# Layer modulation and gates on VectorE: two contraction tiles by 1024 columns at a time, with the sums over partitions two ticks later

## The chip, the cores and the metric

One Trainium2 chip, of which the kernel uses one core. The metric is device time in microseconds (us) of one execution. Engines are called by their profile names: PE (TensorE matmul), PEld (its weight load), DVE (VectorE), ACT (ScalarE), POOL (GpSimd), SP (the queue that issues most loads).

## The reference, cut to what matters

The model has two layers over 256 tokens of width 2048, all in float32. Each layer takes a shift, a scale and a gate from one conditioning vector, and uses them so (only the latent path is shown; the context path has its own first-layer modulation):

```python
def modulation(cond, w, b, n):
    m = jax.nn.silu(cond) @ w[:, :n * D_MODEL] + b[:n * D_MODEL]
    return jnp.split(m, n, axis=-1)

for i in range(DEPTH):
    sh, sc, gt = modulation(c_lat, w_ada[i], b_ada[i], 3)
    u = x * (1.0 + sc) + sh
    y = even_mixer(u @ w_in_e, ...) if i == 0 else odd_mixer(u @ w_in_o, ...)
    x = layer_norm(alpha * x + gt * y, ln_g[i], ln_b[i])
```

`w_ada` has 2048 rows (the contraction) and 6144 columns per layer: shift, scale, gate, 2048 each. A product with a single vector uses each weight once, so it is 16 MB of loads per section and little arithmetic.

## The kernel before, in words

The heavy products run as three matmuls each (`mm3`, L188): a weight tile is split by ACT (L152) and DVE (L153) into a high and a low float32r part, so that each 1 MB weight unit costs two ACT casts and two DVE subtractions of 128x1024. Weight units are four contraction tiles of 128 by 512 columns, loaded by SP (`load_unit`, L135) into a ring of four raw buffers of 4 KB per partition; `w_ahead` (L165) loads up to two units ahead and splits one ahead.

The stages, with the times that the profile shows for them: first-layer modulation and keys (0 to 198 us), values V (198 to 276), queries and the first gate (276 to 376), eight convolution blocks (376 to 602; the gated linear attention runs beside them), first output product OE with its layer norm (602 to 718), second layer's product ODD (718 to 903), second output product OO with the last norm (903 to 1004).

Four sections of 2048 columns are the subject here: `c` (second layer's scale), `g` (first layer's gate), `h` (second layer's shift), in this order (`ADA_ORDER`, L34), and after OE the second layer's gate, `gt1` (L1194). None uses PE for the contraction. DVE multiplies a weight tile [128, 512] by the conditioning value of each partition and adds it to an accumulator `aacc` (`ada_accum`, L525): one tensor_scalar (L531) for the first tile, 15 scalar_tensor_tensor (L533) for the rest of a block of 512 columns. A 1 MB unit is four contraction tiles by 512 columns, from the same raw ring, by the same SP queue. When a block of 512 is complete, PE sums over partitions: for `c` and `h` four matmuls against a column of ones (L554) and a bias add on DVE (L293, L295); for the gates a matmul against a matrix of ones (L520) and an add (L521) to a tile `gt` into which POOL loaded the bias when the block began (L513).

Who sets the pace: sections are generators. After each weight unit of a heavy product `tick` (L608) is called; it runs what was deferred to `later`, advances background work, and adds a stage's credit to a counter, and each whole credit advances the front generator by one `yield`:

```python
ada_credit[0] += ada_credit[1]
pump_ada(int(ada_credit[0]))
ada_credit[0] -= int(ada_credit[0])
```

Credits per tick are 3 in V (6 ticks), 0.4 in the 16 ticks of queries and first gate, 0.8 in the 32 ticks of the convolution blocks, 1 in OE (12 ticks before its last block) and 0.55 in ODD (36 ticks). A block of 512 columns has five yields, four of which each load a unit; a section has four blocks, so 20 yields. ODD's ticks come in this order: g0 (4), x0 (4), x1 (4), p0 (1), x2 (4), p1 (1), x3 (4), p2 (1), g1 (4), p3 (1), g2 (4), g3 (4). Blocks x take 20 matmuls per tick, the others 24.

`cols_ab` (L1133) and the line after `drain()` at the end of ODD (L1334) force what is left; `add` in `ln_blocks` (L1078) forces the gates that it needs. The order of instructions on each engine is set at build time by a list scheduler that goes by program order as priority and by modelled durations, so an instruction can stand some way from its place in the program; at run time each engine keeps its order and waits at the head of its queue. Most large tiles share one pool `s4` of `NSLOT` = 31 slots of 4 KB per partition; `gt` is one of them, `aacc` is not (a pool of its own, two buffers of 2 KB).

Of the kernel before, what the change touches and what calls it, by code (L numbers as in the profile page):

```python
# [21 lines left out]
NSLOT = 31  # L22
# [4 lines left out]
ADA_SLOT = None  # L27
ADA_PE = ((), ())
# [7 lines left out]
ADA_PRIO = 0  # L36
# [10 lines left out]
ADA_ENG = ("v", "v", "v", "v")  # L47
# [13 lines left out]
def kernel(  # L61
# [403 lines left out]
    def ENG(names):  # L465
        return names and [{"v": nc.vector, "g": nc.gpsimd}[n] for n in names]

# [10 lines left out]
    def ada_unit(layer, k0, n0):  # L478

        if not ADA_SLOT:  # L480
            r = load_unit(w_ada[layer], k0, 4, n0)
            return [r[:, j, :] for j in range(4)]
        q = {"s": nc.sync, "g": nc.gpsimd}[ADA_SLOT]
        parts = []
        for k in (k0, k0 + 2):
            r = slot([P, 2, 512], F32, "araw")
            q.dma_start(r, w_ada[layer][k * P : (k + 2) * P, n0 : n0 + 512].rearrange("(k p) n -> p k n", p=P))
            parts += [r[:, 0, :], r[:, 1, :]]
        return parts

    def ada_acc_gen(layer, n0, hold):
        ps = mp([P, 512], "adl")
        for k0 in range(0, KT, 4):
            r = ada_unit(layer, k0, n0)
            for j in range(4):
                nc.tensor.matmul(
                    out=ps[32 * j : 32 * j + 32, :], lhsT=sil[:, k0 + j, 2:34], rhs=r[j],
                    start=k0 == 0, stop=k0 == KT - 4)
            if k0 < KT - 4:
                yield  # L500
        hold.append(ps)
        yield
# [3 lines left out]
    def ada_rows_gen(layer, dst, engs):  # L506

        for nb in range(4):
            if nb % 2 == 0:
                dst.append(slot([P, 2, 512], F32, "gt"))  # L510
            g = dst[nb // 2][:, nb % 2, :]
            n0 = 2 * D + nb * 512
            nc.gpsimd.dma_start(g, b_ada[layer : layer + 1, n0 : n0 + 512].to_broadcast([P, 512]))  # L513
            a = small([P, 512], "aacc1")
            for k0 in range(0, KT, 4):
                ada_accum(ada_unit(layer, k0, n0), k0, a, engs)
                if k0 == KT - 4:
                    yield
                    pb = mp([P, 512], "gtb")
                    nc.tensor.matmul(out=pb, lhsT=ones, rhs=a, start=True, stop=True)  # L520
                    nc.vector.tensor_tensor(out=g, in0=pb, in1=g, op=ALU.add)  # L521
                    gt_done.setdefault(id(dst), set()).add(nb)
                yield

    def ada_accum(r, k0, a, engs):  # L525
        e = engs[(k0 // 4) % len(engs)]
        with prio(ADA_PRIO):
            for j in range(4):
                sc = sil[:, k0 + j, 2:3]
                if k0 + j == 0:  # L530
                    e.tensor_scalar(out=a, in0=r[j], scalar1=sc, scalar2=None, op0=ALU.mult)  # L531
                else:
                    e.scalar_tensor_tensor(out=a, in0=r[j], scalar=sc, in1=a, op0=ALU.mult, op1=ALU.add)  # L533

    def ada_cols_gen(layer, n0, dst, bias, one, engs, on_pe=()):

        for nb in range(4):
            ns = slice(4 * nb, 4 * nb + 4)
            if nb in on_pe:
                hold = []  # L540
                for _ in ada_acc_gen(layer, n0 + nb * 512, hold):
                    if not hold:
                        yield
                add_bias(dst[:, ns], to_cols(hold[0], 512)[:, :, 0], bias[:, ns], one)
                yield
                continue
            a = small([P, 512], "aacc1")
            for k0 in range(0, KT, 4):
                ada_accum(ada_unit(layer, k0, n0 + nb * 512), k0, a, engs)
                yield  # L550
            yield
            pt = mp([P, 4], "adaS")
            for q in range(4):
                nc.tensor.matmul(out=pt[:, q : q + 1], lhsT=a[:, q * P : (q + 1) * P], rhs=ones[:, 0:1], start=True, stop=True)  # L554
            add_bias(dst[:, ns], pt, bias[:, ns], one)

    gt0, gt1 = [], []
    jobs = {
        "c": lambda: ada_cols_gen(1, D, scT1, bT[1][:, 16:32], True, ENG(ADA_ENG[0]), ADA_PE[0]),
        "h": lambda: ada_cols_gen(1, 0, shT1, bT[1][:, 0:16], False, ENG(ADA_ENG[1]), ADA_PE[1]),  # L560
        "g": lambda: ada_rows_gen(0, gt0, ENG(ADA_ENG[2])),
# [39 lines left out]
    later = []  # L601

    def flush():
        now, later[:] = later[:], []
        for f in now:
            f()
# [464 lines left out]
    def ln_blocks(src, order, getu, res, gt, budget, after, before=None, between=None, halves=False):  # L1071
# [3 lines left out]
        def add(nb, m, cs=slice(0, 512)):  # L1075
            if nb not in rt:
                rt[nb] = res(nb)
            while ada_bg and not (len(gt) > nb // 2 and nb in gt_done.get(id(gt), ())):  # L1078
                pump_ada(1)
# [107 lines left out]
    def x1_gen():  # L1187
        for nb in range(4):
            for row, op in ((ln_g[0], ALU.mult), (ln_b[0], ALU.add)):
                t = bcast_row(row, nb)  # L1190
                nc.vector.tensor_tensor(out=rt[nb], in0=rt[nb], in1=t.unsqueeze(1).to_broadcast([P, 2, 512]), op=op)
                yield 1200

    ada_bg.append(ada_rows_gen(1, gt1, ENG(ADA_ENG[3])))  # L1194
    ada_credit[1] = ADA_1
    B = 2500

# [183 lines left out]
```

## Time and profile before

| what | value |
|---|---|
| runs of the kernel, median (lowest to highest) | 1011.63 us (1009.72 to 1018.11), 3 runs |
| the profiled execution | 1005.89 us |
| its span of instructions | 1004.1 us |
| granted TensorE clock, mean | 0.995 |

The profile is of one execution. Its span is 1.8 us shorter than that execution's time; the execution itself is 5.7 us below the median. Matmuls are pipelined and their ends are modelled, so a PE that shows as fully busy can still have small holes.

### The profile page before, as it was taken

What the parts mean: (1) busy time and instruction counts of PE and PEld (TensorE: products, weight loads), DVE (VectorE), ACT (ScalarE), POOL (GpSimd) and SP (SyncE); (2) the same over time, 40 slices, a digit from 0 to 9 for tenths busy, and PEclk for the clock granted to TensorE, in tenths of its full rate; (3) what the DMA queues carried; (4) which work ended last, traced back from release to release, by engine and by line L of the source; (5) the groups of instructions that cost most, each with busy time, mean ns of one, the idle gap of its engine ahead of it and who ended that gap; (6) DMA issues with size and microseconds to landing.
All of it is one profiled execution on the core that took longest, in us unless ns stands there. A gap on an engine that the chain in (4) does not pass through costs nothing.

```text
span 1004.1 us, 14346 instructions
## 1 busy us (share of the span) xinstructions
PE 958.9 (95%) x5654; PEld 757.0 (75%) x5654; DVE 807.0 (80%) x1172; ACT 468.9 (47%) x643; POOL 24.4 (2%) x56
## 2 busy tenths in 40 slices
PE   5899999999999999999999999999989999989995
PEld 4566756778878877877888788888778777768885
DVE  1555646989996999799999879997979997666676
ACT  2422214356675676246463344345745555435340
POOL 2000000000000000000000000000010001000000
PEclk9999999999999999999999999999999999999998
DMA  9987899567787586757766897985598998875532
GB/s 264 328 263 257 289 290 339 188 242 235 260 300 262 179 268 218 257 195 258 248 215 226 299 309 263 327 303 200 175 354 288 309 333 317 264 282 190 178 117 84
DMA packets 150371, 255.44 MB, mean 254 GB/s; under 512 B 5078, under 2 KB 46720, under 8 KB 150304
## 3 DMA queue, kind: packets, MB, share of 16 engines
q1 hardware_dynamic: 146592, 245.13, 72.5%
q0 software_dynamic: 2896, 8.72, 2.9%
q8 instruction: 44, 0.72, 0.3%
q10 hardware_dynamic: 816, 0.68, 0.3%
q14 instruction: 23, 0.19, 0.0%
HBM read 252.41 MB, written 2.10 MB: 253 GB/s over the span
## 4 chain that ended last, share of the span: by engine, by line
PE 49%; DVE 29%; DMA 15%; issue 4%; ACT 2%; SPq 0%; DVEq 0%; ACTq 0%
DMA raw<-in_w_ada_dram 12%; DVE wl L153 10%; DVE aacc L533 7%; PE oacc L190 5%; PE oacc L191 5%; PE oacc L192 5%; PE xacc L192 5%; PE xacc L191 5%; PE xacc L190 5%; PE ada L274 2%; DMA raw<-in_w_in_o_dram 2%; PE kacc L190 2%; PE kacc L192 2%; PE kacc L191 2%; PE pr L405 1%
## 5 line engine op out<-in xcount | busy, mean ns | idle before, releaser
L152 ACT CAST wh<-raw 128x1024 fp32r<-128x1024 f32 (+1 forms) x250 | 257.2, 1044 | 249.4 <-PE xacc L192 74.5
L153 DVE TENSOR_TENSOR wl<-raw,wh 128x1024 fp32r<-128x1024 f32 (+1 forms) x250 | 298.0, 1210 | 46.7 <-ACT wh L152 44.2
L533 DVE SCALAR_TENSOR_TENSOR aacc<-raw,sil,aacc 128x512 f32<-128x512 f32 x240 | 179.3, 747 | 30.8 <-DMA raw<-in_w_ada_dram 27.1
L190 PE MATMUL xacc<-wh,uxh 128*128 128x512 f32 x384 | 152.6, 397 | 0.0
L192 PE MATMUL xacc<-wh,uxl 128*128 128x512 f32 x384 | 151.5, 395 | 0.0
L191 PE MATMUL xacc<-wl,uxh 128*128 128x512 f32 x384 | 150.2, 391 | 0.5 <-DVE wl L153 0.4
L191 PEld LDWEIGHTS xacc<-wl,uxh 128*128 128x128 f32 x384 | 72.2, 188 | 16.3 <-DVE wl L153 1.3
L190 PEld LDWEIGHTS xacc<-wh,uxh 128*128 128x128 f32 x384 | 72.1, 188 | 15.5 <-ACT wh L152 0.5
L192 PEld LDWEIGHTS xacc<-wh,uxl 128*128 128x128 f32 x384 | 72.1, 188 | 15.3 <-issue 0.2
L425 DVE TENSOR_TENSOR knat<-kacc,knat 128x512 f32<-128x512 f32 x64 | 42.8, 685 | 34.7 <-PE kacc L192 34.5
L285 ACT COPY arow<-ada 128x256 f32<-128x256 f32 (+1 forms) x9 | 3.1, 349 | 100.6 <-PE ada L274 100.6
L274 PE MATMUL ada<-raw,sil 128*32 128x256 f32 (+1 forms) x576 | 36.2, 382 | 10.8 <-DMA raw<-in_w_ada_dram 10.8
L190 PE MATMUL xacc<-wh,u1h 128*128 128x512 f32 x112 | 44.9, 401 | 0.8 <-ACT u1h L1160 0.8
L190 PE MATMUL oacc<-wh,y1h 128*128 128x512 f32 (+1 forms) x120 | 45.5, 379 | 0.0
L191 PE MATMUL xacc<-wl,u1h 128*128 128x512 f32 x112 | 44.7, 399 | 0.5 <-DVE wl L153 0.4
L192 PE MATMUL oacc<-wh,y1l 128*128 128x512 f32 (+1 forms) x120 | 45.0, 375 | 0.0
L191 PE MATMUL oacc<-wl,y1h 128*128 128x512 f32 (+1 forms) x120 | 45.0, 375 | 0.0
L192 PE MATMUL xacc<-wh,u1l 128*128 128x512 f32 x112 | 44.5, 397 | 0.0
L274 PEld LDWEIGHTS ada<-raw,sil 128*32 128x32 f32 x576 | 17.4, 118 | 27.0 <-issue 12.0
L190 PE MATMUL kacc<-wh,uxh 128*128 128x512 f32 x64 | 26.8, 418 | 1.5 <-ACT uxh L397 1.5
L1221 PE MATMUL xacc<-wh,dm 128*128 128x512 f32 x64 | 25.7, 402 | 2.5 <-ACT wh L152 2.5
L190 PE MATMUL kacc<-wh,uch 128*128 128x512 f32 x64 | 26.4, 412 | 0.5 <-DVE knat L425 0.5
(339 smaller groups left out, 1866.6 us busy)
## 6 DMA issues: line engine op xcount, KB each, us to landing
raw<-in_w_ada_dram SPq DMA_DIRECT2D x96, 1024.0 KB, 6.3
raw<-in_w_in_e_dram SPq DMA_DIRECT2D x54, 1024.0 KB, 5.5
raw<-in_w_in_o_dram SPq DMA_DIRECT2D x32, 1024.0 KB, 7.2
raw<-in_w_out_e_dram SPq DMA_DIRECT2D x16, 1024.0 KB, 7.0
raw<-in_w_out_o_dram SPq DMA_DIRECT2D x16, 1024.0 KB, 5.1
raw<-in_w_in_e_dram SPq DMA_DIRECT2D x18, 512.0 KB, 7.0
raw<-in_w_pool_dram SPq DMA_DIRECT2D x4, 1024.0 KB, 7.7
gt<-in_b_ada_dram POOLq DMA_DIRECT2D x8, 256.0 KB, 4.1
```

The source lines that it names most:

```text
L152: nc.scalar.copy(h, r[:, j : j + w, :])
L153: nc.vector.tensor_tensor(out=l, in0=r[:, j : j + w, :], in1=h.bitcast(F32), op=ALU.subtract)
L190: nc.tensor.matmul(out=acc, lhsT=uh, rhs=wh, start=start, stop=False)
L191: nc.tensor.matmul(out=acc, lhsT=uh, rhs=wl, start=False, stop=False)
L192: nc.tensor.matmul(out=acc, lhsT=ul, rhs=wh, start=False, stop=stop)
L274: nc.tensor.matmul(out=ps[32 * g : 32 * g + 32, :], lhsT=sil[:, kt, 2 - 2 * half : 34 - 2 * half], rhs=r[:, j, :], start=half == 0 and kt ...
L285: arow_ins.append(nc.scalar.copy(a[:, :nw], ps))
L405: nc.tensor.matmul(out=pr[32 * g : 32 * g + 32, :], lhsT=wr[:, kk, :], rhs=quad_u[kk // 2][:, kk % 2, :], start=True, stop=True,)
L425: nc.vector.tensor_tensor(out=dst, in0=acc, in1=dst, op=ALU.add)
L533: e.scalar_tensor_tensor(out=a, in0=r[j], scalar=sc, in1=a, op0=ALU.mult, op1=ALU.add)
L1221: nc.tensor.matmul(out=accs[0], lhsT=dh, rhs=wh, start=f, stop=False)
```

## The change

The four sections are rewritten. A unit is two contraction tiles by 1024 columns instead of four by 512 (the same 1 MB, the same ring and queue), and DVE works on 128x1024 at a time. A section is two halves of 1024 columns with eight units and eight yields each, 16 yields instead of 20; the credits are unchanged. When a half is complete, its sums over partitions are put off by two ticks (two weight units): `finish` then issues, for a gate, the slot for `gt`, both bias loads on POOL, both matmuls and both adds; for a scale or shift, eight matmuls and one bias add. The accumulator is now one 4 KB slot of `s4`, and `NSLOT` goes from 31 to 32. `ada_end` replaces the forcing at L1135 and L1334, and `add` waits for `gt_done` by running `flush` once the generators are exhausted. The other removed functions (`ada_unit`, `ada_acc_gen` and their options) were not used with the options set.

```diff
-NSLOT = 31
+NSLOT = 32
...
+    def after_ticks(n, f):
+        later.append(f if n == 0 else lambda: after_ticks(n - 1, f))
...
+    def ada_section(layer, n0, finish):
+
+        for half in range(2):
+            c0 = n0 + half * 1024
+            a = slot([P, 1024], F32, "aacc")
+            for k0 in range(0, KT, 2):
+                r = load_unit(w_ada[layer], k0, 2, c0, 1024)
+                for j in range(2):
+                    sc = sil[:, k0 + j, 2:3]
+                    if k0 + j == 0:
+                        nc.vector.tensor_scalar(out=a, in0=r[:, j, :], scalar1=sc, scalar2=None, op0=ALU.mult)
+                    else:
+                        nc.vector.scalar_tensor_tensor(out=a, in0=r[:, j, :], scalar=sc, in1=a, op0=ALU.mult, op1=ALU.add)
+                if k0 == KT - 2:
+                    ada_open[0] += 1
+                    after_ticks(2, lambda half=half, a=a: finish(half, a))
                 yield
...
+    def ada_end():
+        pump_ada(1000)
+        while ada_open[0]:
+            flush()
+
+    def ada_rows_gen(layer, dst):
+
+        def finish(half, a):
+            dst.append(slot([P, 2, 512], F32, "gt"))
+            for i in range(2):
+                nb, g = 2 * half + i, dst[half][:, i, :]
+                n0 = 2 * D + nb * 512
+                nc.gpsimd.dma_start(g, b_ada[layer : layer + 1, n0 : n0 + 512].to_broadcast([P, 512]))
+                pb = mp([P, 512], "gtb")
+                nc.tensor.matmul(out=pb, lhsT=ones, rhs=a[:, i * 512 : (i + 1) * 512], start=True, stop=True)
+                nc.vector.tensor_tensor(out=g, in0=pb, in1=g, op=ALU.add)
+                gt_done.setdefault(id(dst), set()).add(nb)
+            ada_open[0] -= 1
+
+        return ada_section(layer, 2 * D, finish)
+
+    def ada_cols_gen(layer, n0, dst, bias, one):
+
+        def finish(half, a):
+            ns = slice(8 * half, 8 * half + 8)
+            pt = mp([P, 8], "adaS")
+            for q in range(8):
                 nc.tensor.matmul(out=pt[:, q : q + 1], lhsT=a[:, q * P : (q + 1) * P], rhs=ones[:, 0:1], start=True, stop=True)
             add_bias(dst[:, ns], pt, bias[:, ns], one)
+            ada_open[0] -= 1
+
+        return ada_section(layer, n0, finish)
```

## Rows read from the trace of the kernel before

**Rows 1.** The page's first part: busy us, share of span, instructions of each engine.
```profile
PE 958.9 (95%) x5654; PEld 757.0 (75%) x5654; DVE 807.0 (80%) x1172; ACT 468.9 (47%) x643; POOL 24.4 (2%) x56
```

**Rows 2.** Windows by stage: length, PE, PEld, DVE, ACT, POOL, clock, DMA share, GB/s.
```profile
198.00:276.00 78.00, 77.58 (x353) 63.84 (x352) 71.63 (x104) 46.66 (x72) 0.51 (x5) 1.00 0.73 251
276.00:376.00 100.00, 98.39 (x740) 79.44 (x739) 91.03 (x118) 68.39 (x82) 1.41 (x5) 1.00 0.75 252
376.00:602.00 226.00, 220.46 (x1588) 179.40 (x1588) 206.43 (x319) 110.13 (x148) 3.96 (x6) 1.00 0.74 247
602.00:690.00 88.00, 87.62 (x408) 72.54 (x407) 80.54 (x109) 37.59 (x43) 0.00 (x0) 1.00 0.83 291
718.00:903.00 185.00, 176.69 (x786) 143.11 (x785) 152.87 (x187) 93.14 (x114) 10.10 (x20) 0.99 0.88 302
...
940.00:960.00 20.00, 20.00 (x90) 16.57 (x89) 12.11 (x15) 7.74 (x8) 0.00 (x0) 1.00 0.60 191
```

**Rows 3.** The same windows, tile aacc alone: length, PE, PEld, DVE, clock, DMA, GB/s.
```profile
198.00:276.00 78.00, 2.85 (x24) 3.15 (x24) 35.62 (x50) 1.00 0.73 251
276.00:376.00 100.00, 1.97 (x10) 1.42 (x10) 18.83 (x26) 1.00 0.75 252
376.00:602.00 226.00, 4.19 (x14) 1.94 (x14) 58.40 (x80) 1.00 0.74 247
602.00:690.00 88.00, 2.95 (x24) 2.98 (x24) 23.30 (x32) 1.00 0.83 291
...
718.00:903.00 185.00, 3.14 (x6) 0.97 (x6) 46.78 (x64) 0.99 0.88 302
```

**Rows 4.** Waits of PE: us in total, times, longest us.
```profile
PE yT L968 <- DVE y L962: 4.1, 3, 2.0
PE y1T L1279 <- DVE gate L1326: 3.3, 1, 3.3
...
PE xacc L1221 <- ACT wh L152: 2.5, 1, 2.5
...
PE gtb L520 <- DVE aacc L533: 0.3, 1, 0.3
...
PE adaS L554 <- DVE aacc L533: 0.2, 1, 0.2
```

**Rows 5.** Groups of DVE by form: count, busy us, mean ns, idle before and releaser.
```profile
L153 DVE TENSOR_TENSOR wl<-raw,wh 128x1024 fp32r<-128x1024 f32 x246 | 295.3, 1219 | 45.9 <-ACT wh L152 43.4
L533 DVE SCALAR_TENSOR_TENSOR aacc<-raw,sil,aacc 128x512 f32<-128x512 f32 x240 | 179.3, 747 | 30.8 <-DMA raw<-in_w_ada_dram 27.1
L425 DVE TENSOR_TENSOR knat<-kacc,knat 128x512 f32<-128x512 f32 x64 | 42.8, 685 | 34.7 <-PE kacc L192 34.5
...
L531 DVE TENSOR_SCALAR aacc<-raw,sil 128x512 f32<-128x512 f32 x16 | 7.7, 479 | 9.6 <-DMA raw<-in_w_ada_dram 9.6
```

**Rows 6.** Timeline of DVE, then of PE, late in ODD: start, us, idle before.
```profile
881.28 0.75 DVE L533 SCALAR_TENSOR_TENSOR aacc<-raw,sil,aacc 128x512 f32<-128x512 f32 x1 [4.46 <-DMA raw<-in_w_ada_dram]
...
883.08 1.22 DVE L1326 TENSOR_TENSOR gate<-gate,pooled 128x1024 f32<-128x1024 f32 x1
...
884.35 1.09 PE L1279 MATMUL y1T<-ident,gate 128*128 128x128 f32 x8 [3.31 <-DVE gate L1326]
```

**Rows 7.** Window behind that wait (columns of rows 2).
```profile
885.50:888.80 3.30, 3.30 (x9) 2.61 (x8) 3.30 (x5) 0.46 (x2) 0.00 (x0) 0.50 0.76 263
```

**Rows 8.** The bias loads of the gates, line 513, in its source view.
```profile
DMA to landing us min/median/max: 3.6/4.1/5.8
```

**Rows 9.** A window in ODD with blocks x (columns of rows 2).
```profile
820.00:840.00 20.00, 20.00 (x94) 16.65 (x93) 15.34 (x20) 10.59 (x13) 3.20 (x6) 1.00 1.03 376
```

**Rows 10.** Issues of 725 to 745, then of the whole span: count, size, median landing.
```profile
raw<-in_w_in_o_dram SPq DMA_DIRECT2D x3, 1024.0 KB, 11.1
...
raw<-in_w_out_o_dram SPq DMA_DIRECT2D x16, 1024.0 KB, 5.1
```

More of the change, by code (lines that the diff above doesn't have):

```diff
@@ L26 @@
 ADA_V = 3
-ADA_SLOT = None
-ADA_PE = ((), ())
 HALVES = True
@@ L35 @@
 ADA_O = 1
-ADA_PRIO = 0
 ADA_C = 0.8
@@ L46 @@
 SPLIT_0 = 2
-ADA_ENG = ("v", "v", "v", "v")
 WIDE_E = 2
@@ L463 @@
     ada_credit = [0.0, 0.0]
-    def ENG(names):
-        return names and [{"v": nc.vector, "g": nc.gpsimd}[n] for n in names]
     ada_bg = []
@@ L476, in pump_ada @@
                 ada_bg.pop(0)
[L478 to L499, printed above, removed]
-                yield
-        hold.append(ps)
-        yield
-    gt_done = {}
[L506 to L553, printed above, removed]
+    later = []
@@ new lines, in flush @@
+    def flush():
+        now, later[:] = later[:], []
+        for f in now:
+            f()
+    def after_ticks(n, f):
+        later.append(f if n == 0 else lambda: after_ticks(n - 1, f))
+    gt_done = {}
+    ada_open = [0]
+    def ada_section(layer, n0, finish):
[13 more added lines that the diff above has]
+                    after_ticks(2, lambda half=half, a=a: finish(half, a))
+                yield
@@ L554, in ada_cols_gen @@
+    def ada_cols_gen(layer, n0, dst, bias, one):
[3 more added lines that the diff above has]
+            for q in range(8):
                 nc.tensor.matmul(out=pt[:, q : q + 1], lhsT=a[:, q * P : (q + 1) * P], rhs=ones[:, 0:1], start=True, stop=True)
             add_bias(dst[:, ns], pt, bias[:, ns], one)
+            ada_open[0] -= 1
+        return ada_section(layer, n0, finish)
     gt0, gt1 = [], []
     jobs = {
-        "c": lambda: ada_cols_gen(1, D, scT1, bT[1][:, 16:32], True, ENG(ADA_ENG[0]), ADA_PE[0]),
@@ L560 @@
-        "h": lambda: ada_cols_gen(1, 0, shT1, bT[1][:, 0:16], False, ENG(ADA_ENG[1]), ADA_PE[1]),
-        "g": lambda: ada_rows_gen(0, gt0, ENG(ADA_ENG[2])),
+        "c": lambda: ada_cols_gen(1, D, scT1, bT[1][:, 16:32], True),
+        "h": lambda: ada_cols_gen(1, 0, shT1, bT[1][:, 0:16], False),
+        "g": lambda: ada_rows_gen(0, gt0),
     }
@@ L599, in drain @@
             pump(1e9 if gen is None else 1)
[L601 to L606, printed above, removed]
     def tick(budget):
@@ L1077, in add @@
                 rt[nb] = res(nb)
-            while ada_bg and not (len(gt) > nb // 2 and nb in gt_done.get(id(gt), ())):
-                pump_ada(1)
+            while nb not in gt_done.get(id(gt), ()):
+                if ada_bg:
+                    pump_ada(1)
+                else:
+                    flush()
             t = small([P, 512], "arow")[:, cs]
@@ L1134, in cols_ab @@
         ln_exp_tables()
-        pump_ada(1000)
+        ada_end()
         nc.vector.tensor_tensor(out=A1, in0=lngT, in1=scT1, op=ALU.mult)
@@ L1192, in x1_gen @@
                 yield 1200
-    ada_bg.append(ada_rows_gen(1, gt1, ENG(ADA_ENG[3])))
+    ada_bg.append(ada_rows_gen(1, gt1))
     ada_credit[1] = ADA_1
@@ L1333 @@
     drain()
-    pump_ada(1000)
+    ada_end()
     ada_credit[1] = 0.0
```

## The prediction

> **What bounds the kernel now.** I read the page's busy line first: PE 95%, DVE 80%, PEld 75% [rows 1]. An average over stages doesn't say which engine ends last, so next come the windows by stage [rows 2]. Look at PE against the length: it is busy for 77.58 of 78 us in V, 98.39 of 100 in the queries, 220.46 of 226 in the convolutions, 87.62 of 88 in OE, 176.69 of 185 in ODD. In these five stages PE stands idle for 0.4 + 1.6 + 5.5 + 0.4 + 8.3 = 16.2 us. DVE is nearly as full until the end of OE (92%, 91%, 91%, 92%) and at 83% in ODD. So PE ends the stages, and DVE matters where it makes PE wait.
>
> Ends of matmuls are modelled, so I checked the holes by PEld too. In the window of OO where 90 matmuls fill 20 us, PEld shows 16.57 us, 82.9% [rows 2]: that is its full pace. The five stages show 63.84, 79.44, 179.40, 72.54 and 143.11; divided by 0.829 that is 77.0, 95.8, 216.4, 87.5 and 172.6 us, which leaves 1.0, 4.2, 9.6, 0.5 and 12.4, together some 28 us. That is an estimate, since small matmuls have another ratio, and it is the ceiling of what any relief can bring in these stages. The list of PE's waits shows that no single one is large; the waits for DVE are 4.1 us at L968, 3.3 at L1279 [rows 4].
>
> **The change part by part.**
>
> *DVE's work.* Before: 240 scalar_tensor_tensor at 747 ns and 16 tensor_scalar at 479 ns, 179.3 + 7.7 = 187.0 us [rows 5]. After: 120 and 8 of twice the width. No row shows that width for this operation; its nearest rows are the tensor_tensor at 685 ns for 512 and 1219 for 1024 columns [rows 5], so 512 more columns cost 534 ns and the wide one 747 + 534 = 1281. At worst it is twice 747, 1494, and nothing is won; at best it costs like the tensor_tensor, 1219. For the tensor_scalar the ends are 479 and 479 + 534 = 1013; I take 746, the middle. Sum: 120 x 1.281 + 8 x 0.746 = 159.7 us, 27.3 us less (ends: 0 and 37).
>
> *Where these 27 us fall.* This decides. A pump advances one yield, and before one yield in five loaded nothing; now each loads a unit. The credits give 6 x 3 = 18 pumps in V, 16 x 0.4 = 6.4 to the end of the first gate, 32 x 0.8 = 25.6 to the end of the convolutions: 50 before OE. Before, c, g and h took 60, so 10 pumps, 8 units, were left for OE: its window indeed shows 32 of the 192 operations, 23.30 us [rows 3]. After, they take 48, so nothing is left for OE. Ahead of OE the aacc operations of the windows take 35.62 + 18.83 + 58.40 = 112.9 us for 156 operations [rows 3]; with the four that ran before 198 us (some 2.7), 115.6. After, all 48 units stand there: six halves of 15 x 1.281 + 0.746 = 20.0 us, 119.8. So DVE has 4 us more to do up to OE, not less, and the relief of 23 us lands in OE, where PE is idle for 0.4 us and where PEld leaves 0.5. I count 0 ahead of OE (bounds -3 and +4: fewer operations at queue heads against 4 us more work) and -0.4 in OE.
>
> *ODD.* 36 ticks x 0.55 = 19.8 pumps. Before, 20 yields: the last unit is loaded by pump 19, tick 35 of 36. After, the sixteenth by tick 30 (16 / 0.55 = 29.1), inside g2. Late in ODD the timeline shows what the old pace costs: DVE stands 4.46 us at an aacc operation whose load hasn't landed, the multiplication of the gate (L1326) is queued behind it and runs at 883.08, and PE waits 3.31 us for it at 884.35 [rows 6]. Behind this the granted clock is 0.50, the lower level of 1.2 GHz, for 3.30 us in which PE does half [rows 7]: 1.65 us. With no unit after tick 30, this place has no aacc operation: -5.0. It can come back if another unit stops an earlier gate in the same way, then 0. What is late next there is the split of g3's weights. The 7 us of DVE work saved in ODD (64 operations at 46.78 us [rows 3] against 40) don't lower its load per tick, as units come 25% faster.
>
> *Waiting for weights.* DVE idles 27.1 + 9.6 = 36.7 us for loads of w_ada [rows 5]. There are 64 units before and after, so as many occasions; I take 0. Rows of 4 KB instead of 2 KB may land faster or not; a quiet 1 MB load takes 5.1 us [rows 10], and if a tenth of that fell away on the 13 occasions it would be 13 x 0.5 = 6.5 us of DVE's idle time. Bounds -3 and +3, value 0.
>
> *Sums over partitions.* The same matmuls, two ticks later. PE waited 0.3 and 0.2 us for them [rows 4]: -0.5 at most, taken with the rest. Bias adds of c and h fall from eight to four.
>
> *Bias loads.* POOL's two loads per gate half now stand directly before the adds that need them, not a block ahead. They land in 4.1 us [rows 8]. If the scheduler puts the add where it thinks the load done, an add may stand at DVE's head, with weight splits behind it and PE behind those. There are four such places: 0 to 4 x 4.1 = 16.4. POOL is busy 2% [rows 1] and splits run ahead of PE; I take +1.
>
> *Slots.* aacc now uses one slot of s4, two while a finished half waits, and one slot is added; gt takes its slots later. In V this is one slot less for the gate work at times. Bounds 0 and +4 (PE's wait for late attention results, L968, doubled [rows 4]); I take 0.
>
> Sum: 0 - 0.4 - 5.0 - 0.5 + 1 = -4.9. Against the profiled execution, 1005.9 - 4.9 = 1001.0; that execution lies 5.7 below the median of the runs shown, so for the median 1011.6 - 4.9 = 1006.7 us.
>
> **The rivals.**
>
> *DVE's time comes back.* For it: DVE is over 90% full in four stages, PE's largest waits are for DVE. Against it: the pace hands the saving to OE. If the scheduler packs the sections so that half of the ceiling of 28 us is recovered, it gives -14: 997.6. The Trainium skill, page Perfetto Trace Analysis, section Identifying the Most-Contended Engine, says to optimize the engine with the highest occupancy, and to judge PE by its weight loads, since its matmul row misleads. By that rule it is DVE, at 80% against 75%, that bounds this kernel, and a cut of 27 us would be the right one. The trace agrees only in part: PEld's full pace here is 82.9%, so PE stands at 75/82.9 = 91% of its own [rows 1, 2].
>
> *The loads become the bound in ODD* (the other side). A tick of a block x lasts 20 x 20/90 us = 4.44 us at PE's pace [rows 2] and now carries 1.55 MB units (1.625 MB) instead of 1.44 (1.510): 366 GB/s instead of 340, before the layer norm rows that POOL loads. The busiest window moved 376 at a DMA share of 1.03 [rows 9], and when the loads crowd, a weight unit takes 11.1 us instead of 5.1 [rows 10]. It decides once the weight units land later than the two units of lead, 2 x 4.44 us. Then PE waits at the head of an x block as it did once at L1221, 2.5 us [rows 4], in all four x blocks, and the units for the gate slip to the end again so that the 5 us stay: +10 to +12, 1022.5. Against it: only 16 of 36 ticks are so dense.
>
> *The bias loads stop DVE*: half of 16.4 us reaches PE, +8 - 5, 1014.6.
>
> *Nothing happens* (the stall moves to an earlier gate): 1011.6.
>
> **How the numbers follow.** Forecast 0.47, DVE's time comes back 0.27, loads bound 0.13, bias loads 0.07, nothing 0.06. The forecast's own range is -9 to 0, 1002.6 to 1011.6. With both other ends in it: 994 to 1021. A measurement of this kernel can tell about 1%, 10 us. Faster by more: most of the second case and a little of the first, 0.28. Slower by more: most of the third, part of the fourth, 0.16. The rest, 0.56.
>
> **What would show it.** Right: scalar_tensor_tensor of 128x1024 near 1281 ns; no aacc operation in OE, DVE there some 23 us less busy with PE as before; the last aacc operation before 880 and no wait of PE for L1326 in g2; DVE's aacc time before OE at 120 us. Wrong: PE's idle time ahead of OE falls by more than 5 us (DVE's time came back), waits of PE for wh or wl in blocks x grow and landings there pass 10 us (loads), or DVE idles at L521 for a bias that hasn't landed (bias loads).

## The result, and the profile after

The changed kernel takes 1022.03 us (median of ten runs, 1019.02 to 1025.05) against 1010.97 (1006.87 to 1018.11) for the kernel before on the same chip: a ratio of 1.0108, with a 95% interval of 1.0089 to 1.0127. It is 11 us slower. The forecast was 1006.7 us with a range up to 1021; both sign and range were missed. Runs 1, 4 and 15 below had one execution each of 1.6 to 3.4 ms, which their medians and ratios leave out.

The page's first part after the change (before: [rows 1]):

```profile
PE 964.4 (95%) x5654; PEld 761.0 (75%) x5654; DVE 785.1 (77%) x1040; ACT 474.6 (47%) x645; POOL 24.4 (2%) x56
```

DVE's groups by form (before: [rows 5]) show that the arithmetic of the operations came as worked out: 1276 ns where 1281 was taken, 745 where 746 was. Together 153.0 + 6.0 = 159.0 us against 179.3 + 7.7 = 187.0 before.

```profile
L149 DVE TENSOR_TENSOR wl<-raw,wh 128x1024 fp32r<-128x1024 f32 x246 | 295.6, 1220 | 100.4 <-ACT wh L148 96.1 <-PE xacc L1199 0.4
L497 DVE SCALAR_TENSOR_TENSOR aacc<-raw,sil,aacc 128x1024 f32<-128x1024 f32 x120 | 153.0, 1276 | 11.9 <-DMA raw<-in_w_ada_dram 11.3
...
L495 DVE TENSOR_SCALAR aacc<-raw,sil 128x1024 f32<-128x1024 f32 x8 | 6.0, 745 | 0.0
```

So DVE was relieved by 28 us of these operations (22 us on the page, 807.0 to 785.1, which counts the overlapping ends of neighbouring operations once), its idle time for loads of w_ada fell from 36.7 to 11.3 us, and the kernel is slower. The idle time of the weight splits (L149, waiting for ACT's half of the split) rose from 43.4 to 96.1 us; a relieved engine waits more, so that alone doesn't say that weights come later. Where PE lost time the windows by stage show (columns and stretches of [rows 2]; the last two rows are the stretches behind 276 us in which the clock was lower):

```profile
198.00:276.00 78.00, 76.31 (x340) 62.23 (x339) 66.73 (x75) 46.08 (x71) 0.51 (x5) 1.00 0.73 251
276.00:376.00 100.00, 91.92 (x642) 74.39 (x641) 91.84 (x108) 62.67 (x75) 0.30 (x3) 0.95 0.78 265
376.00:602.00 226.00, 223.05 (x1662) 180.57 (x1661) 213.16 (x293) 116.78 (x153) 5.07 (x8) 1.00 0.79 269
602.00:690.00 88.00, 88.00 (x406) 73.44 (x405) 57.56 (x67) 36.27 (x38) 0.00 (x0) 1.00 0.64 217
718.00:903.00 185.00, 171.77 (x750) 137.93 (x749) 149.41 (x160) 91.27 (x114) 11.04 (x21) 0.97 0.86 301
281.70:285.10 3.40, 3.40 (x10) 2.62 (x9) 3.40 (x5) 0.00 (x0) 0.00 (x0) 0.50 0.95 336
291.95:298.75 6.80, 4.91 (x11) 3.42 (x12) 6.80 (x9) 6.80 (x12) 0.10 (x1) 0.50 0.81 274
```

In the second row PE is busy 6.5 us less than before (98.39), at a clock of 0.95 instead of 1.00; in ODD 4.9 us less (176.69), at 0.97 instead of 0.99. The last two rows are where the first loss sits, between 276 and 299 us. And the tile aacc alone, in the first five windows (columns of [rows 3]):

```profile
198.00:276.00 78.00, 1.84 (x16) 1.94 (x16) 34.22 (x28) 1.00 0.73 251
276.00:376.00 100.00, 1.84 (x16) 1.94 (x16) 22.70 (x19) 0.95 0.78 265
376.00:602.00 226.00, 5.60 (x24) 3.38 (x24) 61.95 (x50) 1.00 0.79 269
602.00:690.00 88.00, 1.84 (x16) 1.94 (x16) 0.00 (x0) 1.00 0.64 217
718.00:903.00 185.00, 3.76 (x8) 1.51 (x8) 39.88 (x32) 0.97 0.86 301
```

OE holds no unit any more and its DVE is 23 us emptier with PE as full as before, as forecast. Ahead of OE the three windows add to 118.9 us (forecast 119.8).

To see where time is lost I compared the start of the same matmul (the k-th of its kind) in two profiles. A second profile of the kernel before (run 8) lies 2.4 to 2.6 us behind the first at each of the marks from 270 to 719 us; the offset stays the same, so differences between stages are good to some 0.3 us up to there. In ODD it wavers by 3 us. Positive is later than the first profile of before, in us (that execution lies 5 us below the median of its kernel, which is to be added where a mark is set beside a time); the columns are named by the mark's time there:

| kernel | 270, first query matmul | 289, queries | 602, OE starts | 719, ODD | 878, late in ODD | 910, OO | units in OE / ODD |
|---|---|---|---|---|---|---|---|
| before, second profile | 2.4 | 2.4 | 2.5 | 2.6 | 5.2 | 2.9 | 8 / 16 |
| after | -0.3 | 14.1 | 8.9 | 7.3 | 18.3 | 14.0 | 0 / 16 |

Two losses stand there: 14.4 us at the step from V to the queries, of which the stages up to OE give 5 back, and 11 us in ODD, of which 4 come back at its end. PE's waits name what ended them:

```profile
PE xacc L187 <- DVE wl L149: 5.6, 3, 3.7
PE y1T L1255 <- DVE gate L1293: 4.9, 1, 4.9
PE xacc L1197 <- ACT wh L148: 4.8, 2, 2.5
PE xacc L186 <- ACT wh L148: 3.4, 1, 3.4
...
PE y1T L1255 <- DVE gate L1302: 1.0, 1, 1.0
```

**The first loss.** DVE's timeline at V's start (start, us, idle before): DVE stands 12.10 us for a weight, and only behind it comes the first operation of the accumulator, at 212.95; before it was at 189.62.

```profile
207.72 2.59 DVE L149 TENSOR_TENSOR wl<-raw,wh 128x1024 fp32r<-128x1024 f32 x2 [12.10 <-ACT wh L148]
...
212.34 0.69 DVE L750 TENSOR_TENSOR vnat<-vacc,vnat 128x512 f32<-128x512 f32 x1 [1.30 <-PE vacc L188]
212.95 0.74 DVE L495 TENSOR_SCALAR aacc<-raw,sil 128x1024 f32<-128x1024 f32 x1
```

Until then three units of w_ada that SP has issued keep their raw buffers, three of the four, and SP issues one weight unit between 196.02 and 215.04 us. The timeline of SP after the change; of three units in one row the last is issued at the end of the stretch given:

```profile
176.24 19.78 SPq L134 DMA_DIRECT2D raw<-in_w_ada_dram  x3
210.34 0.37 SPq L134 DMA_DIRECT2D raw<-in_w_in_e_dram  x1
...
257.77 7.48 SPq L134 DMA_DIRECT2D raw<-in_w_ada_dram  x3
268.89 0.37 SPq L134 DMA_DIRECT2D raw<-in_w_in_e_dram  x1
272.01 7.52 SPq L134 DMA_DIRECT2D raw<-in_w_ada_dram  x3
281.43 6.94 SPq L134 DMA_DIRECT2D raw<-in_w_in_e_dram  x3
```

The same view before:

```profile
260.53 5.66 SPq L138 DMA_DIRECT2D raw<-in_w_ada_dram  x3
271.98 5.61 SPq L138 DMA_DIRECT2D raw<-in_w_in_e_dram  x3
```

The run of three weight units for the queries starts at 281.43 instead of 271.98, behind three more units of w_ada. What this does to DVE shows from 220 to 300 us, the tile aacc alone, after and then before (columns of [rows 3]):

```profile
220.00:300.00 80.00, 3.68 (x32) 3.88 (x32) 39.02 (x32) 0.94 0.88 299
...
220.00:300.00 80.00, 2.85 (x24) 3.15 (x24) 32.25 (x44) 1.00 0.76 261
```

The accumulator takes 39.02 us of these 80 instead of 32.25, and DVE is busy for 80.00 of 80 us instead of 78.70, so nothing is caught up. PE's timeline at the queries' start:

```profile
280.32 0.50 PE L187 MATMUL xacc<-wl,uxh 128*128 128x512 f32 x1 [3.69 <-DVE wl L149]
...
282.33 0.63 PE L188 MATMUL xacc<-wh,uxl 128*128 128x512 f32 x1
...
292.82 1.22 PE L186 MATMUL xacc<-wh,uxh 128*128 128x512 f32 x2 [3.37 <-ACT wh L148]
295.06 0.79 PE L187 MATMUL xacc<-wl,uxh 128*128 128x512 f32 x1 [1.02 <-DVE wl L149]
```

The waits add to 3.69 + 3.37 + 1.02 = 8.1 us. Behind the first and from within the second the granted clock is 0.50, the lower level of 1.2 GHz, for the two stretches shown above, and the matmuls take 0.63 us instead of 0.39. In these stretches PE is busy for 3.40 + 4.91 = 8.3 us; at half the clock that is 4.2 us more, as an estimate. One half's sums (L530, 1.7 us of PE at 287) stand in this stretch after and in none of it before. Together 14.0 of the 14.4.

**The second loss.** Late in ODD the forecast held: the stall at 881 us [rows 6] is gone, and 4 us of the offset with it. But an earlier gate is now late. DVE's timeline in front of the gate that PE waits 4.9 us for:

```profile
796.59 1.28 DVE L497 SCALAR_TENSOR_TENSOR aacc<-raw,sil,aacc 128x1024 f32<-128x1024 f32 x1
797.80 1.22 DVE L1244 TENSOR_TENSOR zl<-z,zh 128x1024 fp32r<-128x1024 f32 x1
798.94 2.35 DVE L149 TENSOR_TENSOR wl<-raw,wh 128x1024 fp32r<-128x1024 f32 x2
801.21 1.28 DVE L497 SCALAR_TENSOR_TENSOR aacc<-raw,sil,aacc 128x1024 f32<-128x1024 f32 x1
802.40 2.35 DVE L149 TENSOR_TENSOR wl<-raw,wh 128x1024 fp32r<-128x1024 f32 x2
804.67 1.28 DVE L1293 TENSOR_TENSOR gate<-pacc,gate 128x512 f32<-128x512 f32 x2
```

Two operations of the accumulator and two weight units' splits, without a hole, stand ahead of the gate. It is not the only wait: in ODD PE waits 13.3 us in all against 8.2 before, of this 4.8 against 2.5 for the high half of a weight at the head of an x block (L1197; L1221 before), and the clock stands at 0.50 in two stretches of 3.4 and 6.8 us, in which PE is busy for 8.4, against one of 3.3 before [rows 7]. That is some 5.1 us of waits and 2.5 of clock more, as an estimate, for a loss of 6.7.

### The profile page after: what moved, and what is told of

It is laid out like the page before. It is cut to its first block, busy times and chain, and to the rows that moved or that the text cites. A ratio compares the mean times of both kernels' runs of the same rounds, so it can differ in the third digit from the quotient of the medians.

```text
span 1018.1 us, 14233 instructions
## 1 busy us (share of the span) xinstructions
PE 964.4 (95%) x5654; PEld 761.0 (75%) x5654; DVE 785.1 (77%) x1040; ACT 474.6 (47%) x645; POOL 24.4 (2%) x56
## 4 chain that ended last, share of the span: by engine, by line
PE 57%; DVE 25%; DMA 10%; issue 5%; ACT 2%; SPq 0%; DVEq 0%; ACTq 0%
DMA raw<-in_w_ada_dram 7%; DVE aacc L497 7%; DVE wl L149 7%; PE xacc L187 6%; PE xacc L188 6%; PE xacc L186 6%; PE oacc L188 6%; PE oacc L187 6%; PE oacc L186 6%; DMA raw<-in_w_in_o_dram 3%; PE kacc L186 2%; PE kacc L188 2%; PE kacc L187 2%; PE ada L270 2%; PE pr L401 1%
## 5 line engine op out<-in xcount | busy, mean ns | idle before, releaser
L148 ACT CAST wh<-raw 128x1024 fp32r<-128x1024 f32 (+1 forms) x250 | 257.8, 1044 | 263.4 <-PE xacc L188 81.7
L149 DVE TENSOR_TENSOR wl<-raw,wh 128x1024 fp32r<-128x1024 f32 (+1 forms) x250 | 298.3, 1212 | 101.2 <-ACT wh L148 96.9
L497 DVE SCALAR_TENSOR_TENSOR aacc<-raw,sil,aacc 128x1024 f32<-128x1024 f32 x120 | 153.0, 1276 | 11.9 <-DMA raw<-in_w_ada_dram 11.3
L187 PE MATMUL xacc<-wl,uxh 128*128 128x512 f32 x384 | 152.6, 398 | 4.8 <-DVE wl L149 4.7
L187 PEld LDWEIGHTS xacc<-wl,uxh 128*128 128x128 f32 x384 | 73.0, 190 | 21.4 <-DVE wl L149 6.4
L188 PEld LDWEIGHTS xacc<-wh,uxl 128*128 128x128 f32 x384 | 73.0, 190 | 15.3
L270 PE MATMUL ada<-raw,sil 128*32 128x256 f32 (+1 forms) x576 | 36.3, 383 | 10.8 <-DMA raw<-in_w_ada_dram 10.6
L1197 PE MATMUL xacc<-wh,dm 128*128 128x512 f32 x64 | 25.7, 402 | 4.8 <-ACT wh L148 4.8
```

The costliest lines, as they stand in the source:

```text
L148: nc.scalar.copy(h, r[:, j : j + w, :])
L149: nc.vector.tensor_tensor(out=l, in0=r[:, j : j + w, :], in1=h.bitcast(F32), op=ALU.subtract)
L187: nc.tensor.matmul(out=acc, lhsT=uh, rhs=wl, start=False, stop=False)
L188: nc.tensor.matmul(out=acc, lhsT=ul, rhs=wh, start=False, stop=stop)
L270: nc.tensor.matmul(out=ps[32 * g : 32 * g + 32, :], lhsT=sil[:, kt, 2 - 2 * half : 34 - 2 * half], rhs=r[:, j, :], start=half == 0 and kt ...
L497: nc.vector.scalar_tensor_tensor(out=a, in0=r[:, j, :], scalar=sc, in1=a, op0=ALU.mult, op1=ALU.add)
```

## The experiments

The ratio is to the kernel before on the same chip, with its 95% interval. "After" is the changed kernel.

**1. The pace alone: all five credits times 0.8**, so that as many units fall into each stage as before.

```diff
-ADA_V, ADA_O, ADA_C, ADA_X, ADA_1 = 3, 1, 0.8, 0.4, 0.55
+ADA_V, ADA_O, ADA_C, ADA_X, ADA_1 = 2.4, 0.8, 0.64, 0.32, 0.44
```

> The changed kernel with every credit times 0.8 (V 2.4, queries 0.32, convolutions 0.64, OE 0.8, ODD 0.44), so that units come as fast as before the change. Pace theory (18 units instead of 15 in V fill DVE and the raw ring, and the query weights come late): the 14 us that were lost by 290 us go, ratio to the kernel before 0.996 to 1.003. Slot theory (the first accumulator waits for a slot of s4 at the start of V, DVE stands idle from 196 to 208 us and its work then piles up): ratio stays 1.006 to 1.012, first aacc operation still near 213 us.

Measured: 1007.82 us, 0.9983 (0.996 to 1.0007), the time that the pace theory gave.

**2. The accumulator in a pool of its own**, two buffers of 4 KB, and one slot fewer in the common pool.

```diff
-NSLOT = 32
+NSLOT = 31
...
+    aap = ctx.enter_context(tc.tile_pool(name="aap", bufs=2))
...
-            a = slot([P, 1024], F32, "aacc")
+            a = aap.tile([P, 1024], F32, tag="aacc", name=nm("aacc"))
```

> The changed kernel with aacc in a pool of its own (two buffers of 4 KB) and NSLOT 31, credits as they are. Slot theory: first aacc operation near 190 us, the loss by 290 us goes, ratio 0.995 to 1.002. Pace theory: 18 units still in V, ratio 1.005 to 1.011 although the first operation is early.

Measured: 1011.25 us, 1.0007 (0.9982 to 1.0033), the time that the slot theory gave.

**3. Both.**

> Own pool for aacc and credits times 0.8. Either theory: no loss by 290 us, ratio 0.993 to 1.001. If only this one of the three is at or under 1.000, both causes are needed for the loss to go. DVE should be about 20 us less busy up to 602 us than in the kernel before, and if PE gains nothing from it, the ratio is 0.998 to 1.001.

Measured: 1010.33 us, 1.0013 (0.9988 to 1.0039).

**4. The quicker pace in the kernel before**: all its credits times 1.25, so that V gets as many units as after, in narrow operations.

> The kernel before with every credit times 1.25 (V 3.75), so that its 512-column units come at the changed kernel's pace, with its small accumulators. Pace theory: slower by 8 to 15 us, ratio 1.008 to 1.015, PE idle after V. Slot theory: 0.998 to 1.004.

Measured: 1017.37 us, 1.007 (1.0044 to 1.0097), between the two theories' times and nearer to the pace theory's. Its profiled execution, 1023.05 us, is the slowest of its six, so its marks are some us late.

**5. Only V's credit**, from 3 to 2.4.

> The changed kernel with the credit of V alone at 2.4 (14 units in V instead of 18), all other credits as they are. If the jump of 14 us after V is the whole cause, ratio 0.994 to 1.000; if the blocks x of ODD cost their share as well (8 us between 760 and 810 us, 4 us given back at the end), ratio 0.999 to 1.003 and PE still idles some 8 us more than before between 760 and 810.

Measured: 1013.92 us, 1.0038 (1.0013 to 1.0063).

The same marks for these five:

| kernel | 270 | 289 | 602 | 719 | 878 | 910 | units in OE / ODD |
|---|---|---|---|---|---|---|---|
| 1, pace | -4.2 | -0.7 | -5.6 | -5.2 | 0.5 | 2.0 | 8 / 16 |
| 2, own pool | -1.6 | 3.8 | -0.3 | -1.9 | 7.5 | 3.1 | 0 / 16 |
| 3, both | -2.3 | -0.4 | -2.8 | -0.4 | 4.1 | 5.6 | 9 / 16 |
| 4, before, quick | 5.6 | 13.5 | 15.4 | 12.1 | 23.2 | 17.2 | 0 / 16 |
| 5, V's credit | -3.5 | -0.3 | 6.9 | 5.5 | 10.3 | 4.3 | 2 / 16 |

What follows for the first loss: it has two causes, and taking either away cures most of it. With the own pool the step from 270 to 289 costs 5.4 us instead of 14.4, the first operation of the accumulator stands early in DVE's queue again, and the run of three query weights is issued at 274.32; DVE's and SP's timelines:

```profile
189.10 0.74 DVE L496 TENSOR_SCALAR aacc<-raw,sil 128x1024 f32<-128x1024 f32 x1
...
192.09 1.27 DVE L498 SCALAR_TENSOR_TENSOR aacc<-raw,sil,aacc 128x1024 f32<-128x1024 f32 x1
...
262.29 6.61 SPq L135 DMA_DIRECT2D raw<-in_w_ada_dram  x3
274.32 3.62 SPq L135 DMA_DIRECT2D raw<-in_w_in_e_dram  x3
```

With the slower pace the accumulator still starts late, but fewer units stand in front of the query weights (a pair of them starts at 273.23), and the step from 270 to 289 costs 3.5 us instead of 14.4. The quick pace costs the old kernel 7.9 us at the same place, without the late slot. So it is the pace and the slot together. The accumulator's share of DVE from 220 to 300 us goes with it: 32.48 us in run 1 and 32.09 in run 2, as before the change (32.25), but 38.33 in run 4 and 39.02 after. That the slot in the common pool comes free late is inferred from the move in DVE's queue when the pool is changed; which tile held it was not traced.

Run 1 also shows what DVE's relief is worth where the pace is left as it was: PE is 5.6 us ahead of before at OE's start, 4.4 of it gained since V's start, where it was 1.2 ahead. By the end nothing of it is left (2.0 us late at 910). Run 5 lost that: it is 4.8 ahead at 585 us and 6.9 late at OE's start, with a wait of 3.80 us for late attention results (L941) at 590 us between. Why there was not followed up.

Four of the five lose in ODD, from 719 to 910: 7.2, 5.0, 6.0 and 5.1 us; run 5 gains 1.2.

**6. Only ODD's credit**, from 0.55 to 0.44 (the units per tick of before).

> The changed kernel with the credit of ODD alone at 0.44 (units there as fast as before the change). V theory alone: the loss stays, ratio 1.008 to 1.012. If the pace in ODD has its own cost: 1.003 to 1.007, the stall between 780 and 810 us gone, the stall near 880 back.

Measured: 1017.36 us, 1.0073 (1.0042 to 1.0105), between the two ranges given. ODD's loss from 719 to 910 is 2.4 us instead of 6.7 in the profile.

**7. The sums at the next tick**, without the deferral.

```diff
-                    after_ticks(2, lambda half=half, a=a: finish(half, a))
+                    after_ticks(0, lambda half=half, a=a: finish(half, a))
```

> The changed kernel with the sums over partitions issued at the next tick instead of two ticks behind. If the deferral costs (a second accumulator held in s4): ratio under 1.008. If it gains (PE no longer waits for the accumulator): over 1.013. If it is neutral, as PE's waits at L517 and L530 of under 1 us say: 1.008 to 1.013.

Measured: 1031.81 us (four executions), 1.0222 (1.0172 to 1.0272): 10 us slower than after, by the medians. The deferral was taken as worth next to nothing, and it is worth 10 us in this version. By the marks (17.7 us at 289, 18.3 at 602, 21.4 at 910, against 14.1, 8.9 and 14.0 after) most of it is lost between 270 and 602. DVE's waits show part of the cost, here without the deferral:

```profile
DVE shT L291 <- PE adaS L530: 3.3, 2, 2.6
...
DVE scT L289 <- PE adaS L530: 3.0, 2, 2.1
```

and in the changed kernel:

```profile
DVE shT L291 <- PE adaS L530: 0.7, 1, 0.7
```

The add of the bias stands at DVE's head and waits for a sum, which PE runs behind its matmuls; the low half of the next weight is behind that add on DVE. At 290 us the timeline of the run without deferral has the wait in one line:

```profile
290.06 0.17 DVE L289 SCALAR_TENSOR_TENSOR scT<-adaS,colT 128x8 f32<-128x8 f32 x1 [2.12 <-PE adaS L530]
```

Behind it PE waits 0.39 us for that low half, at 298 us. Its longer wait there, 5.52 us, is for the high half, whose cast stands on ACT behind activations that had waited for PE. So how the 10 us come about is shown only in part.

**8. The kernel before, profiled once more.**

> The kernel before once more, for a second profile: how far two executions differ by stage. The times by stage should agree within 2 us up to 700 us; in ODD they tell whether the 5 to 7 us that every changed version lost there against the first profile are more than the spread of the kernel before.

One run of 1008.78 us; its marks are in the first table. They differ by 2.4 to 2.6 us up to 719, where 2 had been expected, by 5.2 at 878 and by 2.9 at 910, so a change of 3 us within ODD in one profile says little.

**9 and 10. The pace of run 1 ahead of ODD, ODD's credit left at 0.55**; the second with the own pool as well.

> After with the four credits ahead of ODD times 0.8 (V 2.4, X 0.32, C 0.64, O 0.8) and ODD's left at 0.55: differs from the run with all credits times 0.8 in ODD alone. Theory A (the credit of ODD decides its loss: 5 quarters of the units per tick crowd weights and gates): PE is 5 us ahead of the kernel before at OE's start, as with all credits slowed, and loses some 14 us by 809 as the changed kernel did, of which 4 come back at 880: +6 at the end, 1016 us, ratio 1.005. Theory B (what stands late in ODD follows from where the units fall against the gates, and the quicker pace empties the last gate): loss in ODD near -1, as in the run with V alone slowed: -5 to -6 at the end, 1005 us, ratio 0.995.

> The same credits (V 2.4, X 0.32, C 0.64, O 0.8, ODD 0.55) and the accumulator in a pool of its own, 31 slots in the other. If theory A of ODD holds: as the run with 0.44 and own pool in the earlier stages, then a loss of 10 or more in ODD, 1018 us, ratio 1.007. If theory B holds: 1005 to 1008 us, ratio 0.995 to 0.998. The own pool should change nothing in V, where the pace alone has already removed the loss.

Measured: 1011.14 us, 1.0005 (0.9985 to 1.0024), and 1010.6 us, 0.9989 (0.9971 to 1.0007). Neither theory's time came: in both, ODD loses 17 us from 719 to 878 and gets 6 back. In the profiles the quicker credit costs ODD 4 to 5 us in three pairs (after against 6; 9 against 1; 10 against 3). In the times the intervals of each pair overlap, and 10 against 3 points the other way. So the credit in ODD is at most a small part.

**11. The pace of run 1, without the deferral.**

> After with all five credits times 0.8 and the sums over partitions at the next tick. Theory A (the deferral matters only where DVE has no slack: sums wait for the last accumulation, the adds of the bias at the head of DVE wait for the sums, splits stand behind them): with the old pace DVE has slack at these places, so within 3 us of the run with the same pace and the deferral, 1009 to 1012 us, ratio 0.998 to 1.001. Theory B (a sum issued early stops PE itself wherever it falls): some 10 us more, as in the quick version, 1019 us, ratio 1.008.

Measured: 1014.03 us median, ratio 1.0014 (0.9989 to 1.0039), against 0.9983 for run 1: 3 us more by the ratio, with intervals that overlap. That is just above the 1.001 to which the first theory went and well under the 1.008 of the second. So with the old pace the deferral is worth some 3 us or nothing, in the quick version 10; that DVE's slack makes the difference is argued, not shown.

**12 to 14. Units out of ODD.** OE has room after the change. The gate's sixteen units are queued from OE's start on, behind the others; three versions, on the own pool (12: credit 0.5 in OE and 0.25 in ODD) and on the slower pace (13: 0.8 and 0.33; 14: 1 and 0.25). `cols_open` counts the halves of `c` and `h` whose sums are still to come.

```diff
+    g1 = ada_rows_gen(1, gt1)
+    ada_bg.append(g1)
     ada_credit[1] = ADA_O
...
-        ada_end()
+        while ada_bg[0] is not g1:
+            pump_ada(1)
+        while cols_open[0]:
+            flush()
...
-    ada_bg.append(ada_rows_gen(1, gt1))
     ada_credit[1] = ADA_1
```

> After with the accumulator in its own pool (31 slots), and the last sixteen units (the second layer's gate) queued from OE's start, credits 0.5 in OE and 0.25 in ODD, so that about half of them stand in OE, where the own-pool run has no such unit, DVE at 66 of 95 us and the DMA share at 0.57. Theory A (ODD's loss is the crowding of its loads and DVE work by sixteen units): ODD's +5 becomes -3 or better, OE loses at most 1: -2 to -4 at the end, 1007 us, ratio 0.997 or below. Theory B (ODD's loss comes from where the gates stand against the splits, whatever the number of units): +3 to +7 stays, 1011 to 1014 us.

> After with V 2.4, X 0.32, C 0.64, O 0.8, and the last sixteen units queued behind the others from OE's start, ODD 0.33: some five of them stand in OE, eleven in ODD. The run with the same pace ahead of OE was 5 us ahead of before at ODD's start and gave 7 back in ODD. Theory A: 11 units of 16 leave 11/16 of these 7, so the end is at -0.5 to -3, 1007 us, ratio 0.996 to 0.999. Theory B: 1010 us, ratio 0.9985, as that run.

> The same with credit 1 in OE and 0.25 in ODD: some eight of the sixteen in OE, eight in ODD; DVE in OE then has 84 + 8 x 1.28 = 94 of 95 us. Theory A: half of ODD's 7 us goes, OE may lose 1 to 3 because DVE is full there: 1005 to 1008 us, ratio 0.995 to 0.998. Theory B: ODD's 7 stay and OE loses 1 to 3: 1011 to 1013 us.

Measured: 1000.56 us, 0.9895 (0.9866 to 0.9924); 1010.06 us, 0.9997 (0.9979 to 1.0014); 1006.67 us, 0.9964 (0.9946 to 0.9981). Run 12 gained more than the 2 to 4 us of its first theory. Run 13 came near the second theory's time, run 14 at the first's, but by another way: OE cost it 16 us, not 1 to 3.

**15 and 16. Which parts are needed**: the move of run 12 without the own pool, and the same move in the kernel before (credit 1 in OE, 0.42 in ODD).

> After (accumulator in the common slots, V 3) with the last sixteen units queued from OE's start, credits 0.5 in OE and 0.25 in ODD: the own-pool version of it without the own pool. Theory (the changed kernel's two losses are independent: 14 us in V by the late slot, of which the later stages give 7 back, and the crowding of ODD): the V loss of some 14 us by 290 stays, ODD's loss goes from +7 to -3: 1010 to 1013 us, ratio 0.999 to 1.002, that is 10 us above the own-pool version. Rival (the own pool matters little once ODD is relieved): 1000 to 1004 us, ratio 0.99.

> The kernel before with its last sixteen units queued behind the others from OE's start (credit 1 in OE, 0.42 in ODD); its OE already holds eight units of the earlier sections, so some five more come into OE and eleven stay in ODD. Theory (the gain of the best version needs the OE that the change has emptied): as the run with eight and five units in OE, no gain, ratio 0.997 to 1.005. Rival (moving units out of ODD alone does it, with the narrow operations too): ratio 0.990 to 0.994.

Measured: 1011.67 us, 1.0011 (0.9986 to 1.0036), as the theory gave, and 1019.15 us, 1.0097 (1.0062 to 1.0132), slower than either side gave.

| kernel | 270 | 289 | 602 | 719 | 878 | 910 | units in OE / ODD |
|---|---|---|---|---|---|---|---|
| 12, own pool, moved | -0.7 | 4.6 | 0.1 | 4.7 | 0.4 | -3.9 | 8 / 8 |
| 13, pace, moved | -0.6 | 2.7 | -1.2 | 6.7 | 11.6 | 7.5 | 13 / 11 |
| 14, pace, more moved | -1.4 | 1.9 | -1.4 | 14.8 | 7.5 | 3.2 | 16 / 8 |
| 15, moved, common slots | 2.0 | 17.5 | 13.0 | 14.5 | 11.8 | 7.5 | 8 / 8 |
| 16, before, moved | 0.6 | 0.6 | 3.1 | 18.4 | 18.7 | 13.6 | 13 / 11 |

ODD's change from 719 to 910 goes with the number of units in it: with eight units -8.6, -11.6 and -7.0 us (12, 14, 15); with eleven +0.8 and -4.8; with sixteen -1.2 to +11.4. OE pays in turn, from 602 to 719: 4.6 and 1.5 us with eight units, 7.9 and 15.3 with thirteen, 16.2 with sixteen. In runs 12 to 15 PE waits there for the layer norm's rows on DVE, 3.8 us with eight units and 4.5 and 6.3 with more; in run 12:

```profile
PE xT L1136 <- DVE xr L1133: 3.8, 2, 2.0
```

Over both stages, from 602 to 910, only the two of these five runs with eight units in each gain: -4.0 us (12) and -5.5 (15), against +8.7 (13), +4.6 (14), +10.5 (16) and +5.1 after. Beside the 66 us of DVE work in OE (run 2) eight units fit; with thirteen or more, OE's cost eats what ODD gains. (In run 16 the mark at 719 lies anywhere from 16 to 29 us by the matmul taken, so only its sum over both stages is good.)

What the units did in ODD is seen best in ACT's casts (L148; L152 before, L149 in run 12), which need only the loaded weight: how long ACT stood for a load of w_in_o, in us and times. First after, then before, then run 12, each from its view of that line from 718 to 903 us:

```profile
  DMA raw<-in_w_in_o_dram: 29.0, 10
```
```profile
  DMA raw<-in_w_in_o_dram: 25.1, 12
```
```profile
  DMA raw<-in_w_in_o_dram: 6.7, 2
```

With eight units fewer the weights are there in time; so they are in run 15 (4.3 us), less so in 14 (10.2). But this wait does not tell why sixteen wide units cost more than sixteen narrow ones: it is 23.5 us in run 1 and 21.7 in run 2, no more than the 25.1 before. The windows of run 12 from 602 to 697 and 718 to 903 (columns of [rows 2]) show PE at 181.71 of 185 us in ODD, where it was 176.69 before and 171.77 after:

```profile
602.00:697.00 95.00, 94.26 (x440) 78.06 (x439) 81.30 (x96) 44.82 (x60) 0.00 (x0) 1.00 0.75 261
718.00:903.00 185.00, 181.71 (x819) 149.36 (x818) 137.43 (x149) 98.70 (x120) 11.03 (x21) 0.99 0.81 273
```

Run 12 beats both kernels. Two of its parts are needed in these runs: without the move the time is that of before (2), without the own pool the loss at V is back (15: PE waits 3.68, 3.37 and 1.01 us at the places where after waits 3.69, 3.37 and 1.02). That the wide operations are needed is not shown. Run 16 has the old pace, so that eight earlier units stand in its OE beside those moved; the quicker pace empties OE with narrow operations too (run 4), and narrow operations at that pace with the move were not run. The pool costs memory for two accumulators more and gives one slot back.

## Why the prediction was wrong

**Right.** The wide operations' durations; 118.9 us of them ahead of OE; OE emptied by 23 us with nothing gained there; the stall at 881 us gone, worth 4 of the 5 us given; bias loads worth nothing visible. They landed in 5.6 us on the page against 4.1 [rows 8], and no wait at the adds of the gates (L518) names a load.

**Failed first: "I count 0 ahead of OE (bounds -3 and +4)".** This took the pumps of all stages ahead of OE as one sum and found 4 us more DVE work in 400 us. But the forecast had itself that V alone gets 18 pumps, each now a unit where one in five was none before. That is 18 units instead of 14.4, with the ring and the queue they share with the weights, in 78 us in which DVE is 92% full. What counts is the order of loads in SP's queue and how much of DVE's work falls into the 80 us around V's end (39.02 us of the accumulator instead of 32.25), not the sum over all stages, which came as worked out. Measured: +8.9 at OE's start, after a loss of 14.4.

**Failed with it: "Slots", value 0, bound +4.** The bound doubled a wait of attention results; the cost came at another place, DVE's queue at V's start, where the accumulator's slot put the first operation 23 us later. A count of slots doesn't show that. Run 2 takes the accumulator out of the common pool, and of the ratio of 1.0108 1.0007 is left.

**Failed third: "-5.0" for ODD.** The -4 at the end came, but the text's own clause, that another unit may stop an earlier gate in the same way, came too and at more than its price of 0: +11 by 878, +6.7 over the stage. In the prediction's terms: 0 ahead of OE became +8.9, -0.4 in OE became -1.6, -5.0 in ODD became +6.7. That is the 14.0 us between the two profiled executions, 11 between the medians. The rival named for the other side (loads as the bound in ODD, 1022.5 us) came nearest in its time, 0.5 us off, and in part of its mechanism for this half: waits at the head of x blocks (4.8 us at L1197) and relief when units are taken out. It had 0.13. Its time is right mostly by chance, as it had nothing of V, the 5 us at the end, which it lets stay, went, and PE waits as long for a gate (4.9 us) as at the x blocks. The range stated, up to 1021, left out this rival's own price.

**Mis-sized: "Sums over partitions", -0.5 at most.** PE's waits of 0.3 and 0.2 us were the price for PE alone; run 7 shows what the two ticks are worth in this kernel, 10 us, with DVE waiting 6.3 us for the sums.

**The rival "DVE's time comes back"** was not wrong in kind: with the pace of before (run 1) PE was 5.6 us ahead by OE, and lost it in ODD. The Trainium skill, page Perfetto Trace Analysis, section Identifying the Most-Contended Engine, would have one optimize the busiest engine; run 1 has DVE's work down by 22 us on its page (807.0 to 785.3) at the old pace, and its ratio of 0.9983 is not told from 1. So in this kernel the trace does not bear out the rule taken alone.

**Open.** Why sixteen units at the old rate per tick still cost ODD 6 to 7 us in runs 1 and 3, in wide operations, when the kernel before carries them. In run 1 PE arrives 5 us early, ACT stands for a load just there, and 4 of the 5 us are gone by 736:

```profile
733.45 1.99 ACT L148 CAST wh<-raw 128x1024 fp32r<-128x1024 f32 x2 [7.40 <-DMA raw<-in_w_in_o_dram]
```

That is not the whole of it: run 3 arrives with 0.4 us and loses as much, and runs 9 and 10 arrive 5 to 6 us ahead and have lost 1 us at most by then. PE's waits in ODD name DVE's queue more than the loads: for gates 6.3 and 5.5 us in runs 1 and 3, for low halves of weights 3.1 and 3.6, against 4.4 and 1.0 before; for high halves at the x blocks 3.5 and 2.7 against 2.5. What puts the gates late there no run told apart.

## What to carry to other kernels

When a pace is given in steps per tick, a change of what a step contains is a change of pace: work out the units per stage and compare each stage's queue of loads and its share of the busy engine, not the total of an engine. Memory that moves from a pool of its own into a shared one can move the first instruction that writes it, and everything behind it in an in-order queue; the profile's start of that first instruction is the thing to look at. And where a change empties a stage, the gain is had only by moving work there: this change lost 11 us as it stood and, with its accumulator apart and eight units moved into the room that its pace had made, won 10.6 (ratio 0.9895).

## What had not been expected of the hardware

A wait of PE can cost more than its length: with the waits of 8.1 us at the queries went two stretches of 3.4 and 6.8 us at a granted clock of 0.50, the lower level of 1.2 GHz, in which the matmuls took 0.63 us instead of 0.39; by the estimate above that is 4.2 us of the loss of 14.4. And 512 more columns of tensor_scalar cost 745 - 479 = 266 ns, half of what they cost in scalar_tensor_tensor (1276 - 747 = 529) and tensor_tensor (1219 - 685 = 534). It reads one tensor, where they read two; no run shows whether that is the reason.
